# Statistic steps of an encoder layer moved along the matmul queue, two MLP products interleaved, one statistic in another PSUM bank

## The chip, the cores and the metric

The kernel runs on one core of one Trainium2 chip. The metric is the device time of one execution in microseconds, as the median of repeated runs. The engines are named as in the profile: PE is TensorE (its weight loads are listed as PEld), DVE is VectorE, ACT is ScalarE, POOL is GpSimd and SP is SyncE, which here only issues transfers.

## What is computed

One layer of an encoder on a sequence of 512 tokens of width 2048, all in float32:

```python
xn = rms_norm(x, attn_norm_g)
u_val, u_gate, q, k, v = split(xn @ w_in)
y_conv = silu(layer_norm(depthwise_conv31(u_val * sigmoid(u_gate)), ln_g, ln_b))
y_na = neighborhood_attention(q, k, v, rpb)          # 16 heads, windows of 8 x 16 on an 8 x 64 grid
mixed = concat([rms_norm(y_conv, conv_out_g), rms_norm(y_na, na_out_g)])
x = x + mixed @ w_out
xn = rms_norm(x, ffn_norm_g)
gate, val = split(depthwise_conv3(xn @ w_up))
x = x + (silu(gate) * val) @ w_down
return rms_norm(x, final_norm_g)
```

So the layer has several statistics over the channels of a token: the first norm, the mean and the variance of the LayerNorm behind the convolution, the norm of the convolution group, that of the attention group, the second norm (ahead of the MLP) and the last one.

## The kernel before, in words

**Layout.** Channels lie on the 128 partitions and tokens on the free axis, so an activation is a list of tiles of 128 x 512. Nearly all of them come from one pool with the tag "t2k" (79 buffers, made by `t2`, L85). A float32 product is taken as three products of rounded parts (`mm3`, L123: high by high, high by low, low by high; L126 to L128). Weights come in units of 128 x 1024: SP loads one (raw, L110), ACT rounds it (whi, L115), DVE takes the rest (wlo, L116). `weights()` keeps three units ahead of the one in use. A unit of an input projection is 24 matmuls of 512 columns.

**Order of the stages.** The input projections come in the order of `ORDER` (L51): convolution channels, values, and eight pairs of heads (first queries, then keys; two units each). Then the output projection runs over the convolution group (`out_half(ma, ...)`, L603), then over the attention group (L712), then the MLP (L845). Its first four hidden blocks use `up_apart` (L778): seven products of 24 matmuls of 256 columns. They are called c0 to c6 here. c6 accumulates in the PSUM bank "po", the others in turn in the three banks "mm". DVE or ACT reads each product out: c0 and c1 at L794, c2 at L796, c3 at L797, c4 at L798, c5 at L801, c6 at L802.

**Steps.** What isn't a big product is written as Python generators, and `tick` (L133) advances each of them by one step at the end of every unit: first those in `steps` (attention, the norms), then those in `asteps` (the convolution group). What a step issues on PE may not stand in PE's queue ahead of the matmul after which the tick was called. On the other engines the tick only gives the step its place in program order.

**Queues.** Each engine works through a fixed queue. The queues are laid down before the run by a planner that goes through time with its own costs and gives each engine the earliest instruction of the program that is ready by then. So a matmul of a statistic stands where the planner thought that its input was there; if the input is later on the chip, PE waits, and all the products behind it wait too. Where a line's first write to a tile of the t2k pool stands, it stands in the order of the program: no tile of that pool is first written ahead of one that the program writes first earlier.

**PSUM.** Eight banks: three "mm", two "tr", one "po", and "sc" with two. "po" takes in turn the attention output (L508), all statistics (L176 and L216), the mean of the convolution group (L398) and c6.

**A statistic** (`rsqrt_steps`, L171): four (times two passes) small matmuls sum the squares over the channels (L183), a short chain on DVE and ACT makes 1/sqrt (L186 to L193), DVE spreads it on two diagonals (dg, L213), and behind one `yield` two matmuls copy it to all partitions (L218) and ACT reads them out (L220).

**The convolution group** (`group_a`, L390) starts when the fifth head pair has been projected. Its steps, one for each unit that follows: two empty steps; the sum of the eight tiles (L394, L396); the mean (L399, L401), subtraction (L404) and squares (L405); an empty step; the matmuls of the variance (name rln); its spreading, then multiplication (L411), Silu (L412), splitting (L413) and squares (L415) of all eight tiles; five empty steps (`RA_AFTER`); the group's norm (name ra) in two steps.

**Attention** (`attention`, L525), for each head pair: a step that loads the bias tables (tab, L460); a step with the values product of the pair before (L514), the scores (L472) and the softmax (L482 to L489, Exp on ACT); three units later the transposes (trp, L499), copied out by ACT (pt, L504).

**The second norm** (`stats2`, L654): SP loads two sums of squares that POOL's transfers accumulated in DRAM (L656, L657); a step later DVE adds them and the statistic rstd2 follows. The MLP blocks multiply by it (L817, L818).

Of the kernel before, what the change touches and what calls it, by code (L numbers as in the profile page):

```python
# [10 lines left out]
F32 = mybir.dt.float32  # L11
F32R = mybir.dt.float32r
AF = mybir.ActivationFunctionType
# [3 lines left out]
P = 128  # L17
D = 2048
S = 512
# [12 lines left out]
NC_ = CONV // P  # L32
NP_ = HEADS // 2
NF = FF // P
U = 8
# [5 lines left out]
H = S // 2  # L41
# [9 lines left out]
ORDER = "aavaav" + "aq" * 4 + "qqqq"  # L51
NORM_AT = 4
NG = GW // 8
RA_AFTER = 5

PCOLS = [("g1", KD), ("dww", NC_ * CK), ("dwb", NC_), ("lng", NC_), ("lnb", NC_), ("cog", NC_),
         ("nag", NC_), ("g2", KD), ("fww", 2 * NF * 3), ("fwb", 2 * NF), ("g3", KD)]
# [9 lines left out]
def layer(ctx: ExitStack, tc: tile.TileContext, xT, xG, w_in, w_v, w_out, w_up, w_down, par, tab, out):  # L67
    nc = tc.nc
# [5 lines left out]
    psm = ctx.enter_context(tc.tile_pool(name="psm", bufs=3, space=bass.MemoryType.PSUM))  # L74
    psa = ctx.enter_context(tc.tile_pool(name="psa", bufs=1, space=bass.MemoryType.PSUM))
# [9 lines left out]
    def t2(name, dt=F32):  # L85
        return tp.tile([P, S], dt, tag="t2k", name=name)
# [11 lines left out]
    def pc(name, i):  # L98
        o = POFF[name] + i
        return prm[:, o:o + 1]  # L100
# [22 lines left out]
    def mm3(ps, w, wk, mh, ml, start, stop):  # L123
        hi, lo = w[:2]
        a = slice(wk * P, (wk + 1) * P)
        nc.tensor.matmul(ps, hi[:, a], mh, start=start, stop=False)  # L126
        nc.tensor.matmul(ps, hi[:, a], ml, start=False, stop=False)  # L127
        return nc.tensor.matmul(ps, lo[:, a], mh, start=False, stop=stop)  # L128
# [4 lines left out]
    def tick(behind):  # L133
        for todo in (steps, asteps):
            while todo:
                try:
                    with tc.issue_after(behind.ins):
                        next(todo[0])
                    break
                except StopIteration:  # L140
                    todo.pop(0)
# [14 lines left out]
    def split(src, g, name):  # L156

        h, l = t2(name + "h", F32R), t2(name + "l", F32R)
        nc.scalar.activation(h, src, AF.Copy, scale=g)
        nc.vector.scalar_tensor_tensor(l, src, g, h.bitcast(F32), op0=ALU.mult, op1=ALU.subtract)  # L160
        return h, l

    def sum_sq(acc, src, first, to=slice(0, S)):
        if first:
            nc.scalar.activation(acc, src, AF.Square)
        else:
            q = t2("sq")[:, to]
            nc.scalar.activation(q, src, AF.Square)
            nc.vector.tensor_add(acc, acc, q)

    def rsqrt_steps(accs, n, name, to=slice(0, S), keep=True, by_token=None):  # L171

        if not isinstance(accs, tuple):
            accs = accs,
        m = (to.stop - to.start) // P
        banks = [psa.tile([P, S], F32, tag="po", name="st")]  # L176
        if len(accs) > 1:
            banks.append(psa.tile([P, 2, S], F32, tag="sc", name="st")[:, 0])
        v, r, y = (sm.tile([P, S // P], F32, tag="rs" + c, name="rs" + c)[:, :m] for c in "vry")
        for b, acc in enumerate(accs):  # L180
            ps = banks[b][:, :m]
            for i in range(m):
                nc.tensor.matmul(ps[:, i:i + 1], acc[:, to.start + i * P:to.start + (i + 1) * P], ones[:, 0:1],  # L183
                                 start=True, stop=True)
            if b:
                nc.vector.scalar_tensor_tensor(v, ps, 1.0 / n, v, op0=ALU.mult, op1=ALU.add)  # L186
            else:
                nc.vector.tensor_scalar(v, ps, 1.0 / n, EPS, op0=ALU.mult, op1=ALU.add)
        nc.scalar.activation(r, v, AF.Sqrt)
        nc.vector.reciprocal(r, r)  # L190
        nc.vector.scalar_tensor_tensor(y, r, -0.5, r, op0=ALU.mult, op1=ALU.mult)
        nc.vector.tensor_mul(y, y, v)
        nc.vector.scalar_tensor_tensor(y, y, 1.5, r, op0=ALU.add, op1=ALU.mult)  # L193

        if by_token is not None:
            by_token.append(y)
# [12 lines left out]
        nc.vector.tensor_sub(yl, y, yh.bitcast(F32))  # L209
        ds = []  # L210
        for part in (yh.bitcast(F32), yl):
            ds.append(t2("dg", F32R))
            nc.vector.tensor_mul(ds[-1].rearrange("p (i k) -> p i k", k=P), ident.unsqueeze(1).broadcast_to([P, m, P]),  # L213
                                 part.unsqueeze(2).broadcast_to([P, m, P]))
        yield
        ps = psa.tile([P, S], F32, tag="po", name="st")  # L216
        for i, dg in enumerate(ds):
            nc.tensor.matmul(ps, ones_r, dg, start=i == 0, stop=i == 1)  # L218
        res = t2(name)
        nc.scalar.activation(res, ps, AF.Copy)  # L220
        return res
# [30 lines left out]
    ps = psa.tile([P, 2, S], F32, tag="sc", name="idle")  # L252
# [22 lines left out]
    for step in ORDER:  # L275
# [5 lines left out]
        i = next(a_ if step == "a" else q_)  # L281
# [106 lines left out]
    ma, ra = [], []  # L388

    def group_a():  # L390
        yield
        yield
        acc = t2("acc")
        nc.vector.tensor_add(acc, ys[0], ys[1])  # L394
        for i in range(2, NC_):
            nc.vector.tensor_add(acc, acc, ys[i])  # L396
        yield
        ps = psa.tile([P, S], F32, tag="po", name="st")  # L398
        nc.tensor.matmul(ps, ones, acc, start=True, stop=True)  # L399
        mu = t2("mu")  # L400
        nc.vector.tensor_scalar(mu, ps, 1.0 / CONV, None, op0=ALU.mult)  # L401
        acc = t2("acc")
        for i in range(NC_):
            nc.vector.tensor_sub(ys[i], ys[i], mu)  # L404
            sum_sq(acc, ys[i], i == 0)  # L405
        yield
        yield
        r = yield from rsqrt_steps(acc, CONV, "rln")
        acc = t2("acc")
        for i in range(NC_):  # L410
            nc.vector.tensor_mul(ys[i], ys[i], r)  # L411
            nc.scalar.activation(ys[i], ys[i], AF.Silu, scale=pc("lng", i), bias=pc("lnb", i))  # L412
            ma.append(split(ys[i], pc("cog", i), "ma"))  # L413
        for i in range(NC_):
            sum_sq(acc, ys[i], i == 0)  # L415
        for _ in range(RA_AFTER):
            yield

        ra.append((yield from rsqrt_steps(acc, CONV, "ra")))


# [125 lines left out]
    p, n = -1, 0  # L547
# [100 lines left out]
    rstd2 = []  # L648
# [5 lines left out]
    def stats2():  # L654
        acc2, q = t2("acc2"), t2("sq")
        nc.sync.dma_start(acc2, sq2[0])  # L656
        nc.sync.dma_start(q, sq2[1])  # L657
        yield
        nc.vector.tensor_add(acc2, acc2, q)
        rstd2.append((yield from rsqrt_steps(acc2, D, "rstd2")))  # L660

    def factors(f):

# [47 lines left out]

    out_half(mb, after)  # L712
    steps.append(stats2())

    def up(f, between):
# [61 lines left out]

    def up_apart(f, between):  # L778

        def product(c):  # L780
            w = weights()
            ps = (psa.tile([P, S], F32, tag="po", name="pu") if c == 6 else
                  psm.tile([P, S], F32, tag="mm", name="pu"))[:, :H]
            for k in range(U):
                m = comb[c][k]
                i = mm3(ps, w, k, m[:, :H], m[:, H:], k == 0, k == U - 1)
            tick(i)
            between(c)
            return ps

        vv, v, uu, g = (t2(n).rearrange("p (i t) -> p i t", i=2) for n in ("vv", "vl", "uu", "g"))
        both = lambda x: x.unsqueeze(1).broadcast_to([P, 2, H])
        for i in range(2):
            nc.scalar.activation(vv[:, i], product(i), AF.Copy)  # L794
        u, u2 = uu[:, 0], uu[:, 1]
        add(v, vv, both(product(2)))  # L796
        nc.scalar.activation(u, product(3), AF.Copy)  # L797
        add(u2, u, product(4))  # L798
        add(v, v, both(u2))
        add(vv[:, 1], vv[:, 1], u2)  # L800
        add(g[:, 0], u, product(5))  # L801
        add(g[:, 1], vv[:, 1], product(6))  # L802
        return tuple(t.rearrange("p i t -> p (i t)") for t in (g, v))
# [54 lines left out]
    n = CH  # L858
# [146 lines left out]
```

## Time and profile before

| what | us |
|---|---|
| time, median of 3 runs | 2044.64 (2043.89 to 2045.69) |
| the profiled execution, its own time | 2047.1 |
| its span, first to last instruction | 2045.3 |
| PE busy | 2025.5 |
| DVE busy | 1672.8 |
| ACT busy | 1035.4 |
| mean granted PE clock | 0.996 |

The span is the time between the first and the last instruction of one profiled execution; 1.8 us of its own time lie outside it. The profile gives a start and a duration for every instruction; an idle time of an engine is put down to what released it. PE's matmuls overlap, so a matmul of 512 columns has a duration of 0.39 us but the next one starts 0.23 us later. A row of the timeline has start, duration, engine, line, operation, out<-in, shape and count, and in square brackets the idle time before it and its releaser.

### The profile page before, as it was taken

To read this page: it belongs to the slowest core of one execution; us is meant where nothing else is said; L and a number is where in the kernel's file an instruction comes from. 1 tells how busy PE (TensorE), PEld (TensorE's weight loads), DVE (VectorE), ACT (ScalarE), POOL (GpSimd) and SP (SyncE) were. 2 spreads that over 40 slices of the span, in tenths; PEclk is the share of its full clock that TensorE was granted. 3 is DMA by queue.
4 is the path that set the end of the run, shared out by engine and by line. 5 is a ranking of instruction groups with operands and counts; after the bars stand their busy time and mean duration, and the time that the engine had idled before them with its cause. 6 is when DMAs were issued, how large, how long until landed. Compare 5 with 4: busy or idle time off the path is not lost.

```text
span 2045.3 us, 28399 instructions
## 1 busy us (share of the span) xinstructions
PE 2025.5 (99%) x10752; PEld 1731.9 (85%) x10752; DVE 1672.8 (82%) x2319; ACT 1035.4 (51%) x1662; POOL 156.2 (8%) x186
## 2 busy tenths in 40 slices
PE   9999999999999999999999999999999999999997
PEld 7888888878888898888888888888888888888887
DVE  7986888878577898888888788788888888889876
ACT  6323234347346555555555555555554555555552
POOL 0000000000001001111111111111111111110110
PEclk9999999999999999999999999999999999999998
DMA  7232333336347435566566565665555566555682
GB/s 254 82 104 91 114 95 103 108 119 216 104 121 178 113 114 144 118 151 145 124 144 144 135 133 145 138 134 142 131 146 143 124 146 146 130 134 127 149 212 83
DMA packets 97209, 275.38 MB, mean 135 GB/s; under 512 B 10928, under 2 KB 11696, under 8 KB 97072
## 3 DMA queue, kind: packets, MB, share of 16 engines
q1 hardware_dynamic: 71712, 227.40, 36.6%
q0 software_dynamic: 25216, 46.15, 15.6%
q8 instruction: 85, 1.39, 0.3%
q14 instruction: 52, 0.43, 0.1%
q10 hardware_dynamic: 144, 0.01, 0.0%
HBM read 218.99 MB, written 54.53 MB: 134 GB/s over the span
## 4 chain that ended last, share of the span: by engine, by line
PE 95%; DVE 2%; ACT 1%; DMA 1%; issue 1%; SPq 0%; DVEq 0%; ACTq 0%
PE pu L723 25%; PE pu L728 13%; PE pd L128 8%; PE pd L126 8%; PE pd L127 8%; PE pj L128 5%; PE pj L127 5%; PE pj L126 5%; PE po L126 3%; PE po L127 3%; PE po L128 3%; PE pv L330 1%; PE pv L332 1%; PE pv L331 1%; PE pu L126 1%; PE pu L128 1%
## 5 line engine op out<-in xcount | busy, mean ns | idle before, releaser
L115 ACT ACTIVATE whi<-raw 128x1024 fp32r<-128x1024 f32 x364 | 384.9, 1059 | 506.2 <-PE pj L127 148.0
L116 DVE TENSOR_TENSOR wlo<-raw,whi 128x1024 fp32r<-128x1024 f32 x364 | 443.9, 1221 | 215.6 <-ACT whi L115 205.9
L723 PE MATMUL pu<-xc,whi 128*128 128x512 f32 x2240 | 574.9, 392 | 0.2 <-ACT pl L735 0.2
L723 PEld LDWEIGHTS pu<-xc,whi 128*128 128x128 f32 x2240 | 409.2, 189 | 74.3 <-ACT pl L735 0.5
L728 PEld LDWEIGHTS pu<-xc,wlo 128*128 128x128 f32 x2240 | 305.6, 190 | 21.9
L728 PE MATMUL pu<-xc,wlo 128*128 128x256 f32 x2240 | 312.3, 282 | 0.0
L128 PE MATMUL pd<-hh,wlo 128*128 128x512 f32 x640 | 249.2, 391 | 0.0
L127 PE MATMUL pd<-hl,whi 128*128 128x512 f32 x640 | 249.2, 389 | 0.0
L126 PE MATMUL pd<-hh,whi 128*128 128x512 f32 x640 | 248.9, 391 | 0.0
L842 POOL DMA_DIRECT2D x2d<-pdc x160 | 139.2, 872 | 1169.6 <-ACT pdc L841 1051.5
L127 PE MATMUL pj<-xl,whi 128*128 128x512 f32 x512 | 200.4, 391 | 0.1
L128 PE MATMUL pj<-xh,wlo 128*128 128x512 f32 x512 | 200.0, 391 | 0.0
L126 PE MATMUL pj<-xh,whi 128*128 128x512 f32 x512 | 198.6, 392 | 0.4 <-ACT xh L267 0.4
L735 ACT ACTIVATE pl<-pu 128x256 f32<-128x256 f32 x280 | 104.4, 382 | 168.6 <-PE pu L723 168.5
L115 ACT ACTIVATE whi<-ws 128x1024 fp32r<-128x1024 f32 x132 | 139.6, 1058 | 76.9 <-PE pu L723 55.3
L384 DVE SCALAR_TENSOR_TENSOR y<-ch,prm,y 128x500 f32<-128x500 f32 (+14 forms) x240 | 173.4, 741 | 4.5
L116 DVE TENSOR_TENSOR wlo<-ws,whi 128x1024 fp32r<-128x1024 f32 x132 | 160.8, 1218 | 19.7 <-ACT whi L115 19.6
L128 PEld LDWEIGHTS pd<-hh,wlo 128*128 128x128 f32 x640 | 120.1, 188 | 28.8 <-DVE wlo L116 3.0
L127 PEld LDWEIGHTS pd<-hl,whi 128*128 128x128 f32 x640 | 120.3, 188 | 25.0
L126 PEld LDWEIGHTS pd<-hh,whi 128*128 128x128 f32 x640 | 120.5, 188 | 21.9
L841 ACT ACTIVATE pdc<-pd 128x512 f32<-128x512 f32 x160 | 93.8, 588 | 84.1 <-PE pd L128 84.1
L126 PEld LDWEIGHTS pj<-xh,whi 128*128 128x128 f32 x512 | 96.0, 188 | 22.3 <-issue 1.7
(188 smaller groups left out, 2911.3 us busy)
## 6 DMA issues: line engine op xcount, KB each, us to landing
raw<-in_w_up SPq DMA_DIRECT2D x176, 512.0 KB, 3.7
raw<-in_w_down SPq DMA_DIRECT2D x88, 512.0 KB, 4.0
x2d<-pdc POOLq DMA_DIRECT2D x160, 256.0 KB, 4.8
raw<-in_w_in SPq DMA_DIRECT2D x60, 512.0 KB, 3.7
raw<-in_w_out SPq DMA_DIRECT2D x32, 512.0 KB, 3.7
raw<-in_w_v SPq DMA_DIRECT2D x16, 512.0 KB, 4.0
tab<-in_tab SPq DMA_DIRECT2D x32, 256.0 KB, 5.1
x<-in_xG SPq DMA_DIRECT2D x16, 256.0 KB, 5.3
```

The source lines that it names most:

```text
L115: i = nc.scalar.activation(hi[:, :n], raw[:, :n], AF.Copy)
L116: j = nc.vector.tensor_sub(lo[:, :n], raw[:, :n], hi[:, :n].bitcast(F32))
L126: nc.tensor.matmul(ps, hi[:, a], mh, start=start, stop=False)
L127: nc.tensor.matmul(ps, hi[:, a], ml, start=False, stop=False)
L128: return nc.tensor.matmul(ps, lo[:, a], mh, start=False, stop=stop)
L330: nc.tensor.matmul(ps, xh, wh[:, f], start=kk == 0, stop=False)
L384: nc.vector.scalar_tensor_tensor(y[:, a:b], h[:, a + j - PAD:b + j - PAD], prm[:, o + j:o + j + 1], y[:, a:b], op0=ALU.mult, op1=ALU.add)
L723: return nc.tensor.matmul(ps, w[0][:, k * P:(k + 1) * P], comb[c][k], start=k == 0, stop=k == U - 1)
L728: nc.tensor.matmul(ps[:, H:], w[1][:, k * P:(k + 1) * P], comb[c][k][:, :H], start=False, stop=False)
L735: nc.scalar.activation(to, ps, AF.Copy)
L841: nc.scalar.activation(t, ps, AF.Copy)
L842: nc.gpsimd.dma_start(xd[d], t, accum_op=ALU.add)
```

## The change

All of it is in the order of steps, save for one bank:

- `group_a`: the two empty steps at the start go. A step's end is put into the loop of subtractions, after the fourth tile. The squares of the finished tiles move into the loop that makes them, and that loop ends a step after every second tile. `RA_AFTER` goes from 5 to 2. The number of steps up to the group's norm stays the same (12).
- `rsqrt_steps` gets two arguments. With `free` its two banks are taken from "sc" in place of "po". `rest` is the number of steps between the first and the second half.
- `stats2`: one more empty step ahead of the statistic, which is called with `free=True, rest=3`.
- `up_apart`: for the first hidden block the first two products are written as seven of eight parts of c0, seven of c1, then the last part of each; the ticks of c0 and c1 stand behind their seventh parts. Reading out c0 and c1 follows both.

```diff
-RA_AFTER = 5
+RA_AFTER = 2
...
-    def rsqrt_steps(accs, n, name, to=slice(0, S), keep=True, by_token=None):
+    def rsqrt_steps(accs, n, name, to=slice(0, S), keep=True, by_token=None, free=False, rest=1):
...
-        banks = [psa.tile([P, S], F32, tag="po", name="st")]
+
+        def bank():
+            if free:
+                return psa.tile([P, 2, S], F32, tag="sc", name="st")[:, 0]
+            return psa.tile([P, S], F32, tag="po", name="st")
+
+        banks = [bank()]
...
-        yield
-        ps = psa.tile([P, S], F32, tag="po", name="st")
+        for _ in range(rest):
+            yield
+        ps = bank()
...
     def group_a():
-        yield
-        yield
         acc = t2("acc")
...
         for i in range(NC_):
             nc.vector.tensor_sub(ys[i], ys[i], mu)
             sum_sq(acc, ys[i], i == 0)
+            if i == NC_ // 2 - 1:
+                yield
         yield
         yield
         r = yield from rsqrt_steps(acc, CONV, "rln")
...
             ma.append(split(ys[i], pc("cog", i), "ma"))
-        for i in range(NC_):
             sum_sq(acc, ys[i], i == 0)
+            if i % 2:
+                yield
         for _ in range(RA_AFTER):
             yield
-
...
         nc.vector.tensor_add(acc2, acc2, q)
-        rstd2.append((yield from rsqrt_steps(acc2, D, "rstd2")))
+        yield
+        rstd2.append((yield from rsqrt_steps(acc2, D, "rstd2", free=True, rest=3)))
...
+        def begin(c):
+            return weights(), (psa.tile([P, S], F32, tag="po", name="pu") if c == 6 else
+                               psm.tile([P, S], F32, tag="mm", name="pu"))[:, :H]
+
+        def part(c, w, ps, ks):
+            for k in ks:
                 m = comb[c][k]
                 i = mm3(ps, w, k, m[:, :H], m[:, H:], k == 0, k == U - 1)
-            tick(i)
+            return i
+
+        def product(c):
+            w, ps = begin(c)
+            tick(part(c, w, ps, range(U)))
             between(c)
             return ps
 
+        def first_two():
+            got = [begin(c) for c in range(2)]
+            for c in range(2):
+                tick(part(c, *got[c], range(U - 1)))
+            for c in range(2):
+                part(c, *got[c], range(U - 1, U))
+            return [ps for _, ps in got]
+
...
-        for i in range(2):
-            nc.scalar.activation(vv[:, i], product(i), AF.Copy)
+        for i, ps in enumerate(first_two() if f == 0 else map(product, range(2))):
+            nc.scalar.activation(vv[:, i], ps, AF.Copy)
```

More of the change, by code (lines that the diff above doesn't have):

```diff
@@ L778, in up_apart @@
     def up_apart(f, between):
[L780 to L784, printed above, removed]
+        def begin(c):
[3 more added lines that the diff above has]
+            for k in ks:
                 m = comb[c][k]
                 i = mm3(ps, w, k, m[:, :H], m[:, H:], k == 0, k == U - 1)
-            tick(i)
+            return i
+        def product(c):
+            w, ps = begin(c)
+            tick(part(c, w, ps, range(U)))
             between(c)
             return ps
+        def first_two():
[5 more added lines that the diff above has]
+            return [ps for _, ps in got]
         vv, v, uu, g = (t2(n).rearrange("p (i t) -> p i t", i=2) for n in ("vv", "vl", "uu", "g"))
         both = lambda x: x.unsqueeze(1).broadcast_to([P, 2, H])
-        for i in range(2):
-            nc.scalar.activation(vv[:, i], product(i), AF.Copy)
+        for i, ps in enumerate(first_two() if f == 0 else map(product, range(2))):
+            nc.scalar.activation(vv[:, i], ps, AF.Copy)
         u, u2 = uu[:, 0], uu[:, 1]
```

## The prediction

> **What bounds the kernel now.** I read the page first, then PE's list of waits, then PE's timeline at the waits that the change touches, and last DVE's and ACT's timeline there.
>
> ```profile
> span 2045.3 us, 28399 instructions
> ...
> PE 2025.5 (99%) x10752; PEld 1731.9 (85%) x10752; DVE 1672.8 (82%) x2319; ACT 1035.4 (51%) x1662; POOL 156.2 (8%) x186
> ```
>
> PE is busy for 99% of the span, and the change takes no product away. It can gain only where PE stands still, and what it can lose is a new standstill. The list of PE's waits (engine, line, releaser; total, times, longest) has six that lie in the changed stretches:
>
> ```profile
> PE st L399 <- DVE acc L396: 1.3, 1, 1.3
> PE st L218 <- DVE dg L213: 1.1, 1, 1.1
> ...
> PE trp L499 <- DVE tab L489: 0.9, 1, 0.9
> PE pu L126 <- ACT xc L612: 0.8, 1, 0.8
> PE pu L126 <- ACT rstd L220: 0.7, 1, 0.7
> ...
> PE st L183 <- DVE acc L659: 0.4, 1, 0.4
> ```
>
> Together 5.2 us, by starts and ends of a matmul's record. What a wait costs is seen better from start to start, since the next matmul normally starts 0.23 us after the last:
>
> ```profile
> 426.19 0.39 PE L126 MATMUL pj<-xh,whi 128*128 128x512 f32 x1
> ...
> 432.31 0.39 PE L126 MATMUL pj<-xh,whi 128*128 128x512 f32 x1
> 434.02 1.10 PE L399 MATMUL st<-acc,ones 128*128 128x512 f32 x2 [1.32 <-DVE acc L396]
> ...
> 478.87 0.39 PE L127 MATMUL pj<-xl,whi 128*128 128x512 f32 x1
> 480.17 0.63 PE L499 MATMUL trp<-ident,tab 128*128 128x128 f32 x4 [0.91 <-DVE tab L489]
> ```
>
> From 426.19 to 432.31 PE starts 27 matmuls, 0.227 us apart; a unit of 24 lasts 5.44 us. The mean's matmul starts 1.71 us after its predecessor, so 1.48 us are lost; the transposes' wait costs 1.30 - 0.23 = 1.07 us. At the second norm:
>
> ```profile
> 691.06 0.28 PE L128 MATMUL pu<-xc,wlo 128*128 128x256 f32 x1
> 692.47 1.01 PE L218 MATMUL st<-dg,ones 128*128 128x512 f32 x2 [1.14 <-DVE dg L213]
> 694.17 0.39 PE L126 MATMUL pu<-xc,whi 128*128 128x256 f32 x1 [0.69 <-ACT rstd L220]
> ```
> ```profile
> 694.17:698.05 3.88, 3.88 (x20) 3.88 (x20) 0.82 (x2) 0.23 (x1) 0.56 0.00 0
> 698.05:720.00 21.95, 21.95 (x185) 21.95 (x184) 2.27 (x5) 1.09 (x3) 1.00 0.31 97
> ```
>
> The second fence is the product tiles by stretches (length, PE, PEld, DVE, ACT, then the granted clock, DMA share, GB/s). The last matmul of c4 gives way at 691.18, and the next product starts at 694.17: 2.99 us, of which the two spreading matmuls need 2 x 0.23. So 2.53 us are lost. Then the clock is granted at 0.56, and 20 matmuls take 3.88 us where the next stretch needs 21.95 / 185 = 0.119 us for one, 2.37 us in all: 1.51 us more. **The second norm loses 4.0 us here**, more than the list of waits says.
>
> **The convolution group.** What it adds up does not grow: the same additions, subtractions, squares and splits, the same 12 steps to the group's norm. Only their places move. PE's first step and DVE before:
>
> ```profile
> 404.58 1.47 PE L499 MATMUL trp<-ident,tab 128*128 128x128 f32 x12
> ```
> ```profile
> 402.75 0.73 DVE L384 SCALAR_TENSOR_TENSOR y<-ch,prm,y 128x497 f32<-128x497 f32 x1
> ...
> 412.14 0.69 DVE L433 TENSOR_TENSOR q<-pj,rstd 128x512 f32<-128x512 f32 x1 [5.28 <-PE pj L128]
> ...
> 419.58 0.68 DVE L394 TENSOR_TENSOR acc<-y 128x512 f32<-128x512 f32 x1
> ...
> 421.38 2.48 DVE L482 SCALAR_TENSOR_TENSOR tab<-sc,tab 128x512 f32<-128x512 f32 x4
> ...
> 431.86 0.68 DVE L489 TENSOR_TENSOR tab<-tab,su 128x512 f32<-128x512 f32 x1
> 432.46 1.41 DVE L396 TENSOR_TENSOR acc<-acc,y 128x512 f32<-128x512 f32 x2
> ```
>
> The convolution is done at 403.5, yet the sum of its tiles starts at 419.58, in the third step, and is squeezed between the softmax until 433.87, past PE's arrival at 432.54. With the two empty steps gone it belongs to the first step, behind the transposes that PE starts at 404.6. DVE then is free for 5.28 us ahead of 412.14; seven additions at 0.6 (their starts in a row) need 4.3. The mean's matmul stands behind the second step, which ends at about 412. I take its wait as 0; at the worst it is what it is now, 1.48, at the best there is no more to gain. The mean's own matmuls cost the same in either place.
>
> What is late next is the sum of squares of the variance. The four subtractions of the second step lie in idle DVE time before the scores; the last four additions share the softmax's stretch, four where there were six, so they end two additions (1.2 us) before 433.87, at 432.7; PE comes to them behind the fifth step, at 432.3 plus the mean's 1.2, 433.5. No wait by 0.8 us, narrowly. The bound is again 1.48.
>
> ```profile
> 447.71 0.95 PE L183 MATMUL st<-ones,acc 128*128 128x1 f32 x8
> ...
> 456.07 0.66 PE L514 MATMUL po<-pt,vg 128*64 128x128 f32 x8
> ...
> 457.97 2.00 PE L472 MATMUL sc<-k,q 64*128 64x256 f32 x16
> ...
> 474.77 0.60 PE L499 MATMUL trp<-ident,tab 128*128 128x128 f32 x4
> ```
> ```profile
> 455.35 0.58 ACT L220 ACTIVATE rln<-st 128x512 f32<-128x512 f32 x1
> 455.95 1.28 ACT L412 ACT_TABLE_LOAD   x1
> ...
> 467.41 1.28 ACT L487 ACT_TABLE_LOAD   x1
> ```
> ```profile
> 479.34 1.28 DVE L489 TENSOR_TENSOR tab<-tab,su 128x512 f32<-128x512 f32 x2
> ```
> ```profile
> 450.46 2.05 SPq L460 DMA_DIRECT2D tab<-in_tab  x4
> ```
>
> The variance moves from 447.71 to about 433.5, rln from 455.35 to about 444. Between 456 and 475 the eight Silus, splits and squares now run ahead of the Exps of a softmax, and PE meets its third transposes late (tab until 480.6). Its scores now end at 459.97; the values product ahead of them waits for rln's read of "po" (455.93), about 1.8 us that go, as do the mean's 1.5, so they end near 456.7. With the Silus done by then, that softmax needs what it needed in the pair before, 421.38 to 432.54, 11.2 us, and some two more for the second half of the splits: ready by 470, where the first transposes are due at 474.77 - 1.5, about 473. The 1.07 us go, with some 3 us to spare. Bounds: nothing gained, 0, and one new pair of table loads, 2 x 1.28, lies inside the spare time. The tables for that softmax (SP, 450.46) now stand behind the first writes of rln and of the first two splits, which by the same reckoning are made by about 450 (rln 444, a table load, two Silus with their splits and squares at some 2 us each): no later than now.
>
> **The second norm.** The second load of `stats2` on SP's queue:
>
> ```profile
> 683.38 0.32 SPq L657 DMA_DIRECT2D sq<-sq  x1
> ```
>
> It is issued when POOL's last accumulating transfer has landed; the step doesn't hold it, so a tick that is three matmuls earlier doesn't move it, and PE's 0.4 us for L659 stay. No transfer is moved past another on SP's or POOL's queue.
>
> The interleaving of c0 and c1:
>
> ```profile
> 674.20:679.24 5.04, 5.04 (x43) 5.04 (x42) 0.00 (x0) 0.00 (x0) 1.00 0.88 235
> ```
>
> 43 matmuls run ahead of the wait for xc, which are 2 x 21 and one of c2: the planner already puts c1's seven parts ahead of c0's last. Writing that order out costs and gains 0; the bounds are the 0.8 us of that wait, gained or lost again.
>
> What counts is `rest=3` and the bank. The spreading matmuls now stand behind c5, 24 matmuls later; DVE's diagonals are long there. c6 no longer shares "po" with rstd2. But c5 needs a bank "mm", which DVE frees by reading c2 (L796):
>
> ```profile
> 692.25 0.68 DVE L213 TENSOR_TENSOR dg<-ident,rsl 128x512 fp32r<-128x512 f32 x1
> ...
> 693.98 0.68 DVE L796 TENSOR_TENSOR vl<-vv,pu 128x512 f32<-128x512 f32 x1
> ```
> ```profile
> 693.52 0.60 ACT L220 ACTIVATE rstd<-st 128x512 f32<-128x512 f32 x1 [1.15 <-PE st L218]
> ```
>
> c2's products had ended two products earlier, yet its reading out starts only behind rstd2's: the order of first writes in the t2k pool. In the new program rstd2 comes behind c5, so L796 follows the second diagonal at about 692.85 and ends at 693.5. Meanwhile PE takes c6. How many of its matmuls stand ahead of c5 is the planner's guess of 1.2 us of DVE work (half of a diagonal and L796), some 10 x 0.12; then PE waits from 691.18 + 1.2 = 692.4 to about 693.6: **1.2 us remain.** Bounds: 0 (c6 whole in front) and 2.4 (none). With a standstill of 1.2 I expect full clock, since behind the mean's 1.48 the clock stays at 1.00:
>
> ```profile
> 436.00:446.00 10.00, 10.00 (x52) 8.41 (x51) 10.00 (x16) 7.15 (x12) 0.00 (x0) 1.00 0.18 52
> ```
> Behind that wait stand c5, the spreading matmuls and the rest of c6, so it costs its full length. Sum here: 4.0 - 1.2 = 2.8 gained. Who waits for the later rstd2 are L817 and L818 and behind them the next block's first copies; c5 ends near 696.5 (24 x 0.12 on) and rstd2 at 697.6, ahead of c6's end, and the banks that are then free last for the next block's first three products, 8.6 us.
>
> **The rule on the clock.** The trace shows half clock after a stretch of 2.99 us in which PE ran only two matmuls, and none after one of 1.48 us. [...]
>
> **The sum.** 1.48 + 1.07 + 2.8 = 5.35 us. Against the profiled execution, 2047.1 - 5.35 = 2041.75 (span 2039.95). It is 2.46 above the median, so of the median 2044.64 remain **2039.3 us**. What a measurement of this kernel can tell from no change is about 0.2%, 4.1 us: the line is at 2040.5.
>
> **The rivals.**
> - *The standstills only move in the group* (14%): the mean's 1.48 reappears at the variance, and the transposes wait as now. For it: DVE's queue between 421 and 434 is full and the planner is optimistic there. Gain 2.8: 2041.8.
> - *The wait for c5's bank takes the place of rstd2's* (9%): PE's queue has c5 at once, waits 2.4 and gets half clock. Gain at the norm 4.0 - 2.4 - 1.5 = 0.1; in all 2.65: 2042.0. Against it: c6 has a free bank and is ready.
> - *The half clock stays whatever the standstill* (7%): 2039.3 + 1.5 = 2040.8. For it: PE wasn't wholly idle in the 2.99 us.
> - *It doesn't do what it says* (3%): the steps give only a lower bound on places, and the queues stay nearly as they are: 2044.6.
> - *No remainder either* (8%): c5's wait goes too: 2038.1.
> - *Slower* (4%): ACT. Silu and Exp each had a table load of 1.28 us, once. The eight Silus now come in four steps; if they alternate with the eight Exps of the softmax behind 456, up to 14 more loads, 17.9 us, less 3 to spare, delay the transposes: 14.9 lost against 4.3 gained, 2055.2. It decides from nine more loads on. Against it: a Silu writes in place and needs only rln, so all eight are ready before the scores. [...]
>
> The forecast has 55%. Its own error of about a microsecond leaves a quarter of it above 2040.5. So **faster** (over 0.2%) is 41 + 8 and some of the third rival, 52%; **slower** 4%; within 0.2% 44%. Range, 8 in 10: from 2037.6 (2038.1 and half a microsecond for the small waits at xc and L659) to 2042.4 (only one of the two parts works, 2041.8 to 2042.0, and some error).
>
> **What would show it.** Right: no wait of PE for L396 near 412; the variance's matmuls near 433 without one; no wait at L499 near 472; L218 of rstd2 behind c5; a wait of some 1.2 us for L796; clock 1.00 throughout 690 to 700; still only one Silu and one Exp load between 440 and 475. Wrong: a row of PE waiting for L169 or L412, more ACT_TABLE_LOAD rows, or a stretch with clock below 1 behind 690.

## The result and the profile after

| | before | after |
|---|---|---|
| median, us (10 runs each) | 2045.62 (2043.89 to 2046.74) | 2040.29 (2038.82 to 2041.88) |
| span of the profiled execution, us | 2045.3 | 2039.1 |

The ratio of the times is 0.9973, with a 95% interval of 0.9965 to 0.9982: 5.3 us less, between 3.7 and 7.2. The forecast was 5.35 us less. As the sections below show, the direction and the stages were right, the mechanism at the second norm was in part wrong, and the size came out so well by luck, because errors in it offset each other.

The lines of the changed file stand 5 to 21 lines lower than before: the mean is L404, the variance L189, the diagonals L219, the spreading matmuls L225, reading out a statistic L227, the transposes L506; c2 is read out at L817 and the second norm's sum is L666.

First the page's span and engines, and then PE's list of waits (engine, tile, line and what it waited for; total, times, longest), both of the changed kernel:

```profile
span 2039.1 us, 28396 instructions
...
PE 2023.6 (99%) x10752; PEld 1730.6 (85%) x10752; DVE 1672.1 (82%) x2319; ACT 1035.5 (51%) x1662; POOL 156.6 (8%) x186
```
```profile
PE rb L210 <- DVE dg L206: 1.9, 1, 1.9
PE idle L261 <- DVE warm L258: 1.6, 1, 1.6
PE st L189 <- DVE acc L169: 0.9, 1, 0.9
PE pu L126 <- ACT xc L619: 0.8, 1, 0.8
PE pu L731 <- ACT pl L743: 0.6, 1, 0.6
PE st L189 <- DVE acc L666: 0.4, 1, 0.4
```

The four waits that the change was after (for L396, L489, L213 and L220 of before) are gone, and no new one is in the list: the others are in before's too. The wait for xc and the one for the second norm's sum have stayed. Two marks divide the span: PE's first matmul of the MLP and its first wide product. They are the first starts in the rows of the tile pu:

```profile
L731 PE MATMUL pu<-xc,whi x2240: 387/389/499, 755.2 to 1953.8; 128*128 128x512 f32 x187
...
L126 PE MATMUL pu<-xc,whi x224: 278/283/386, 671.6 to 754.9; 128*128 128x256 f32 x112
```

| stage, from start to start | before | after | less |
|---|---|---|---|
| **group**: transposes at 404 to the MLP's first matmul | 404.58 to 674.20: 269.62 | 404.16 to 671.61: 267.45 | 2.17 |
| **norm**: the MLP's first matmul to the first wide one | 87.81 | 83.64 | 4.17 |

At the transposes at 404 the changed kernel is already 0.42 us earlier, by a wait for xh at the start that this execution of before had; behind the second mark it loses 0.6 us, at products that are the same in both. The two stages tell where the change works, and the single times and medians don't: the stretch from the first wide product to the last alone took 1197.3 to 1199.5 us over the traces of this study.

In the group, PE's timeline (start, duration, engine, line, out<-in, shape, count), DVE's and ACT's:

```profile
412.43 1.02 PE L404 MATMUL st<-acc,ones 128*128 128x512 f32 x2
...
432.57 0.39 PE L128 MATMUL pj<-xh,wlo 128*128 128x512 f32 x1
432.98 1.02 PE L189 MATMUL st<-ones,acc 128*128 128x1 f32 x8
...
473.05 1.47 PE L506 MATMUL trp<-ident,tab 128*128 128x128 f32 x12
```
```profile
432.16 0.67 DVE L169 TENSOR_TENSOR acc<-acc,sq 128x512 f32<-128x512 f32 x1
...
467.21 0.68 DVE L496 TENSOR_TENSOR tab<-tab,su 128x512 f32<-128x512 f32 x1
```
```profile
443.75 1.28 ACT L419 ACT_TABLE_LOAD   x1
...
458.87 1.28 ACT L494 ACT_TABLE_LOAD   x1
```

The mean has no bracket any more, nor have the transposes, whose table was ready at 467.89, 5.2 us ahead of them. The variance starts 0.41 us after the matmul before it, where 0.23 is usual: its last addition ended at 432.83. Silu and Exp have one table load each.

At the second norm, PE's timeline from the last matmul of c4 to the first of c5, DVE's with ACT's reading of c3 (L818), and the stretch as a whole (length, PE, granted clock, DMA share, GB/s):

```profile
688.45 0.28 PE L128 MATMUL pu<-xc,wlo 128*128 128x256 f32 x1
...
690.13 0.39 PE L225 MATMUL st<-dg,ones 128*128 128x512 f32 x1
...
690.71 0.39 PE L225 MATMUL st<-dg,ones 128*128 128x512 f32 x1
690.93 0.28 PE L127 MATMUL pu<-xc,whi 128*128 128x256 f32 x1
691.05 0.28 PE L126 MATMUL pu<-xc,whi 128*128 128x256 f32 x1
```
```profile
689.03 0.68 DVE L219 TENSOR_TENSOR dg<-ident,rsh 128x512 fp32r<-128x512 f32 x1
689.64 0.68 DVE L219 TENSOR_TENSOR dg<-ident,rsl 128x512 fp32r<-128x512 f32 x1
689.67 0.36 ACT L818 ACTIVATE uu<-pu 128x256 f32<-128x256 f32 x1
690.24 0.68 DVE L817 TENSOR_TENSOR vl<-vv,pu 128x512 f32<-128x512 f32 x1
```
```profile
690.00:694.00 4.00, 4.00 (x34) 1.00 0.08 33
```

Between c4 and c5 stand 13 matmuls of c6, a spreading matmul, three of c6, the other spreading matmul and one of c6. They fill the 2.5 us in which DVE makes the diagonals and reads c2. DVE is no faster than before: the first diagonal starts 4.8 us after the variance's matmuls in both kernels. PE stands nowhere, and the clock stays at 1.00.

### The profile page after: what moved, and what is told of

It reads as the page before. It is cut to its first block, busy times and chain, and to the rows that moved or that the text cites. A ratio compares the mean times of both kernels' runs of the same rounds, so it can differ in the third digit from the quotient of the medians.

```text
span 2039.1 us, 28396 instructions
## 1 busy us (share of the span) xinstructions
PE 2023.6 (99%) x10752; PEld 1730.6 (85%) x10752; DVE 1672.1 (82%) x2319; ACT 1035.5 (51%) x1662; POOL 156.6 (8%) x186
## 4 chain that ended last, share of the span: by engine, by line
PE 97%; issue 1%; DVE 1%; DMA 0%; ACT 0%; POOL 0%; DVEq 0%; ACTq 0%; POOLq 0%; SPq 0%
PE pu L731 25%; PE pu L736 13%; PE pd L128 8%; PE pd L126 8%; PE pd L127 8%; PE pj L126 6%; PE pj L128 6%; PE pj L127 6%; PE po L126 3%; PE po L127 2%; PE po L128 2%; PE pv L339 1%; PE pv L338 1%; PE pv L337 1%; PE pu L128 1%; PE pu L126 1%
```

## The experiments

For each kernel the two stages are given, and two terms of the second one: the waits for xc and for L666 (from start to start, less the usual 0.12), which change from one execution to the next, and the stage without them. Where the table says "under 0.12", nothing is taken off.

| kernel | ratio to before, 95% interval | group | norm | xc | L666 | norm without both |
|---|---|---|---|---|---|---|
| before | | 269.62 | 87.81 | 0.93 | 0.57 | 86.31 |
| after | 0.9973 (0.9965 to 0.9982) | 267.45 | 83.64 | 0.97 | 0.52 | 82.15 |
| e1_group | 0.9988 (0.9979 to 0.9997) | 267.51 | 87.91 | 0.94 | 0.68 | 86.29 |
| e2_norm | 0.9986 (0.9978 to 0.9995) | 269.68 | 82.88 | 0.46 | 0.26 | 82.16 |
| e3_rest1 | 0.9975 (0.9965 to 0.9985) | 267.53 | 85.61 | 0.58 | 1.38 | 83.65 |
| e4_po_bank | 0.9980 (0.9971 to 0.9989) | 267.53 | 84.79 | 1.01 | under 0.12 | 83.78 |
| e5_bank_alone | 0.9973 (0.9963 to 0.9983) | 267.49 | 83.13 | 0.76 | under 0.12 | 82.37 |
| e6_no_step | 1.0008 (0.9999 to 1.0017) | 267.51 | 89.26 | 0.95 | 2.22 | 86.09 |
| e7_three_and_later | 0.9981 (0.9972 to 0.9990) | 267.47 | 85.09 | under 0.12 | under 0.12 | 85.09 |
| e8_light | one run, 2044.42 | 267.46 | 87.31 | 1.02 | under 0.12 | 86.29 |
| e9_all_covered | 0.9979 (0.9970 to 0.9988) | 267.49 | 84.46 | under 0.12 | under 0.12 | 84.46 |
| e10_no_spreading | one run, 2044.02 | 267.88 | 87.02 | 0.80 | under 0.12 | 86.22 |
| e11_only_spreading | one run, 2053.14 | 279.01 | 85.73 | 0.98 | under 0.12 | 84.75 |
| e12_changed_again | 0.9974 (0.9963 to 0.9984) | 267.47 | 83.61 | 0.93 | 0.53 | 82.15 |

### The two parts alone

e1: of the change only the group's part, that is the edits of `RA_AFTER` and `group_a`.

> Only the group's part of the change: the two empty steps gone, squares and Silus spread over steps, RA_AFTER 2; the second norm and the first block's products as before. Theory (two separate parts): the waits of 1.48 and 1.07 us go, less 0.2 to 0.4 that the variance and small changes of the queue take back, as between the two traces: from the transposes at 404 to the first product of the MLP 267.4 us instead of 269.6; then the second norm still stands for 2.99 us with half clock behind it, 87.8 us from the first product to the first wide one. In all 2.2 less than before. Rival (the standstills only move): the stage stays within half a microsecond of 269.6 and the time within 0.5 of before.

e2: only the rest of it, the edits of `rsqrt_steps`, `stats2` and `up_apart`.

> Only the second norm's part: the scores' bank, the longer rest, the extra step, the first two products written out; the group as before. Theory: the 2.53 us of standstill and the 1.51 us of half clock both go and nothing takes their place: 83.6 to 83.8 us from the first product to the first wide one instead of 87.8, and 269.6 from the transposes at 404 to the first product. In all 4.0 to 4.2 less than before. Rival (the prediction's remainder): 1.2 us stay as a wait of c5 for the reading of c2, 85.0 us, 2.8 less in all.

Both hold by their stages. The group's part gives 2.1 us wherever it is (267.45 to 267.53 in all kernels that have the whole of it, 269.62 and 269.68 in the two that lack it), and does nothing to the norm. The norm's part takes 4.15 us off the norm's stage (86.31 to 82.16), and nothing is left of the remainder of 1.2 us; e2's stage is even shorter than the 83.6 to 83.8 expected, because both of its waits happened to be short. By the medians the two parts bring 1.6 and 2.7 us; the intervals are too wide to add to this.

### What carries the gain at the second norm

e3, the rest back at one step:

```diff
-rsqrt_steps(acc2, D, "rstd2", free=True, rest=3)
+rsqrt_steps(acc2, D, "rstd2", free=True)
```

> The changed kernel with rest back at 1. On PE's queue 13 matmuls of c6, a spreading matmul, 3, the other one and 4 more stand ahead of c5 (13, 3 and 1 in the changed kernel). Theory (the bank carries it): with the statistic in the scores' bank c6 need not wait for any reading of it, and fills the time of the diagonals; the rest does nothing. 83.6 to 83.8 us from first product to first wide one, clock 1.00, the time within 0.5 us of the changed kernel. Rival (the rest carries it, as the prediction reasons): the spreading matmuls come back to where they stood, 2.5 us of standstill and 1.5 of half clock come back: 87.8 us for the stage, 4 us more.

e4, the bank back at po:

```diff
-rsqrt_steps(acc2, D, "rstd2", free=True, rest=3)
+rsqrt_steps(acc2, D, "rstd2", rest=3)
```

> The changed kernel with the statistic back in the bank po; rest stays at 3. On PE's queue both spreading matmuls stand right behind c4, then c5, then c6. Theory (the bank carries it): PE waits some 1.1 us for the diagonals and then for the bank of c5 or for rstd2, as before: 2.5 us of standstill, and behind it the clock falls again, 1.5 us: the stage takes 87.0 to 88.2 us, the time is 3.5 to 4.5 us above the changed kernel. Rival (the rest carries it): the stage stays at 83.6 to 84.0 us. Rival on the clock: the standstill is back and the clock stays at 1.00: 86.1 to 86.5 us.

e5, the group's part and the bank alone:

```diff
-        yield
-        rstd2.append((yield from rsqrt_steps(acc2, D, "rstd2", free=True, rest=3)))
+        rstd2.append((yield from rsqrt_steps(acc2, D, "rstd2", free=True)))
...
-enumerate(first_two() if f == 0 else map(product, range(2)))
+enumerate(map(product, range(2)))
```

> The group as in the changed kernel, and of the second norm's edits the bank alone: rest 1, no extra step, the first two products not written out. On PE's queue stand 13 matmuls of c6, a spreading matmul, 3, the other one and 8 more ahead of c5. Theory (the bank carries the gain there): no standstill behind c4 and clock 1.00; the stage from the first product to the first wide one takes 83.6 us, give or take what the wait for L666 happens to be (0.1 to 1.4 us in the runs so far), the time is that of the changed kernel within 0.6 us. Rival (rest, extra step and order are needed too): some of the 2.53 and 1.51 us come back, 85 to 87.9 us.

The timeline behind c4, first in e4, with DVE's reading of c2 (L817), then in e5, with the weight load of c5's first matmul (PEld):

```profile
687.54 0.28 PE L128 MATMUL pu<-xc,wlo 128*128 128x256 f32 x1
688.96 1.01 PE L225 MATMUL st<-dg,ones 128*128 128x512 f32 x2 [1.14 <-DVE dg L219]
689.33 0.68 DVE L817 TENSOR_TENSOR vl<-vv,pu 128x512 f32<-128x512 f32 x1
689.80 0.28 PE L126 MATMUL pu<-xc,whi 128*128 128x256 f32 x1
```
```profile
690.80 0.28 PE L128 MATMUL pu<-xc,wlo 128*128 128x256 f32 x1
691.10 0.19 PEld L126 LDWEIGHTS pu<-xc,whi 128*128 128x128 f32 x1 [0.22 <-ACT uu L817]
691.10 0.39 PE L126 MATMUL pu<-xc,whi 128*128 128x256 f32 x1
```

With the bank po the spreading matmuls stand right behind c4 and wait for the diagonals as before (1.42 us from start to start, 0.12 usual: 1.30), and from the first of them to c5 another 0.84 - 0.45 = 0.39 go, most of it at the second diagonal. That is 1.7 us, and 83.78 - 82.15 = 1.63. With the bank alone, e5, c6 fills this time, and 0.18 us are left at c5, until ACT has read c3 (L817 of e5): 82.37 against 82.15. So the theory of the bank holds: c6's bank is po, and a statistic that takes po too keeps c6 out until ACT has read it. Rest, extra step and written order add only 0.2 us to the bank. But e4 lost less than expected. Its standstill is 1.7 us, not 2.5, because there c5 stands ahead of c6 and needn't wait for the reading of rstd2, and the clock stayed at 1.00. So these three edits without the bank still bring 2.5 us (86.31 to 83.78), 1.5 of them by the clock; the two ways overlap, and the bank alone brings nearly all.

e3's theory holds for the queue, and its stage is 1.5 us too long in another place. Its wait for L666 happened to be 1.38 us, and behind it the clock fell (stretches, columns as above):

```profile
683.40:684.90 1.50, 0.30 (x3) 1.00 0.10 38
684.90:686.70 1.80, 1.78 (x15) 1.00 0.00 0
686.71:690.12 3.41, 3.41 (x18) 0.50 0.81 234
690.12:692.00 1.88, 1.88 (x18) 1.00 0.35 142
```

The half clock doesn't follow the wait at once: PE works for 1.8 us at 1.00 first.

### The order of the first products

e6, the changed kernel without the extra step in `stats2`:

```diff
         nc.vector.tensor_add(acc2, acc2, q)
-        yield
```

> The changed kernel without the extra step in stats2. With the first two products written out, the ticks come earlier, and the variance's matmuls L189 stand 24 matmuls (2.9 us) earlier on PE's queue than in the changed kernel, right behind the first 20 of the third product. Theory (writing the order out is free only with the extra step): PE waits there for L666, 2.9 us longer than the 0.4 of the changed kernel, some 3.3 us, and the clock falls behind it, 1.5 us more: the stage takes 87 to 88 us, the time is 3 to 4.5 us above the changed kernel. Rival (as the prediction has it: a tick that is a few matmuls earlier moves nothing): 83.6 us, no more than half a microsecond above the changed kernel.

```profile
681.76 0.28 PE L128 MATMUL pu<-xc,wlo 128*128 128x256 f32 x1
684.10 1.75 PE L189 MATMUL st<-ones,acc 128*128 128x1 f32 x8 [2.06 <-DVE acc L666]
686.38 0.58 PE L126 MATMUL pu<-xc,whi 128*128 128x256 f32 x1 [0.53 <-ACT whi L115]
...
687.64 0.58 PE L128 MATMUL pu<-xc,wlo 128*128 128x256 f32 x1 [0.47 <-DVE wlo L116]
```

The theory holds, with other sizes. The variance stands 20 matmuls earlier (not 24, as the expectation has it) and waits 2.22 us. Behind it PE takes c6 first, for whose weights it waits another 1.0 us (0.53 and 0.47), and the clock is at a half for 6.8 us, from 684.3 to 691.1. All the gain of the change is lost. So writing out the first two products gains nothing by itself (e5 does without it and is as fast); it moves the ticks, and the extra step in `stats2` is what makes that harmless.

### Whether the clock follows idle time

e8, the second norm's one-column matmuls four times over:

```diff
-            for i in range(m):
+            for i in list(range(m)) * (4 if free else 1):
```

> The changed kernel in which the second norm's eight one-column matmuls (by the trace's count) are done four times over, with the same sums: 24 more at 0.115 us, 2.8 us of PE that is never idle and does hardly any work. Theory (the clock follows what share of some 3.3 us PE's array works): these light matmuls count for little, and about 3.3 us behind their start the clock falls to a half for some 3.4 us: 1.5 us more, so the stage takes 83.6 + 2.8 + 1.5 = 87.9 us. Rival (only idle time counts): the clock stays at 1.00, 86.4 us.

The variance's matmuls in e8 (duration least/median/most in ns, first and last start), and then two stretches of its PE:

```profile
L189 PE MATMUL st<-ones,acc x32: 212/250/313, 683.9 to 687.3; 128*128 128x1 f32 x32
```
```profile
683.97:687.38 3.41, 3.41 (x33) 1.00 0.41 123
687.38:690.80 3.42, 3.42 (x17) 0.50 0.31 73
```

PE is busy without a gap, and the clock falls all the same, from 687.4 to 690.8. The stage without both waits is 86.29: 82.15, the 24 light matmuls (2.7 us), and 1.5. The theory holds in this run: the clock fell behind 3.41 us of one-column matmuls in which PE was never idle. The 3.3 us of the expectation lie between the 3.2 us (e3) and 3.4 us (before, e1) that passed in the traces ahead of it between the standstill and the half clock; here it is 3.5 us.

### The parts of the group

e10, only the two empty steps gone:

> Of the group's edits only the two empty steps are gone; subtractions with squares in one step, Silus and squares in one step, RA_AFTER 5; the second norm as before. The mean stands where it does in the changed kernel, the variance 24 matmuls (5.4 us) earlier than there, ra's statistic 14 us earlier. Theory (the spreading is what keeps the additions from being late): PE waits for the variance's last addition or the softmax behind it is late: of the 2.13 us that the whole part brings, a microsecond or more is lost again, 268.5 us or more from the transposes at 404 to the MLP's first product. Rival (the two empty steps are the whole part): 267.5 us.

e11, only the spreading and `RA_AFTER`:

> Of the group's edits only the spreading and RA_AFTER 2; the two empty steps are kept, the second norm as before. The mean stands where it stood before. Theory (the places of the sums decide): the mean's 1.48 us stay, and the transposes, whose softmax has the later Silus beside it, come no earlier: 269.6 us or up to 1.5 more for the stage. Rival (spreading alone frees the softmax's stretch): the 1.07 us of the transposes go, 268.5 us.

e10's theory falls. The group's stage is 267.88, 0.4 us longer than with the spreading; one wait came in, for rln's diagonals, at which 0.74 us go:

```profile
436.73 0.47 PE L225 MATMUL st<-dg,ones 128*128 128x512 f32 x1 [0.58 <-DVE dg L219]
```

So the two empty steps carry 1.75 of the 2.15 us. e11 is far beyond both expectations: the mean's wait stays, and the stage is 9.4 us longer than before, lost at the group's norm. There PE first waits for the bank po, out of which ACT reads the attention output only behind its Exps, then 2.90 us for the diagonals and 1.41 for the next bank. The row of PE's timeline, and ACT's table loads:

```profile
505.00 1.18 PE L189 MATMUL st<-ones,acc 128*128 128x1 f32 x8 [2.81 <-ACT ao L529]
```
```profile
458.69 1.28 ACT L496 ACT_TABLE_LOAD   x1
462.59 1.28 ACT L421 ACT_TABLE_LOAD   x1
464.79 1.28 ACT L496 ACT_TABLE_LOAD   x1
468.80 1.28 ACT L421 ACT_TABLE_LOAD   x1
```

Here Exp (L496) and Silu (L421) do take turns: the slow rival of the prediction, in a kernel whose Silus come two steps later than in the changed one. The two extra loads are 2.6 us of ACT; how much of the 9.4 us they cause wasn't separated. Part of it is the clock, which is at a half for 10.2 us there, from 505.8 to 516.0.

### Two tries at the waits that stay

e7, three products written out instead of two, and one step more ahead of the variance:

```diff
+        yield
         rstd2.append(...)
...
-            got = [begin(c) for c in range(2)]
+            got = [begin(c) for c in range(3)]
```

> The changed kernel with three products written out in place of two (63 matmuls ahead of the first that needs the last xc, in place of 42) and one step more ahead of the second norm's variance. Theory (both remaining waits are a matter of place): the wait for xc, 0.97 us from start to start, and the one for L666, 0.52, go; 13 to 24 matmuls stand behind where the diagonals are needed, so no new wait comes; the stage takes 82.0 to 82.3 us and the time is 1.4 to 1.5 us below the changed kernel, 6.5 to 7 below the kernel before. Rival (the later statistic is late for the second block): PE waits for a reading that needs rstd2 behind c6, and the stage stays at 83.6 us or longer.

e9, the same with two steps more, rest 1, and c3 in a bank "tr":

> The changed kernel with three products written out, the fourth one's bank taken from tr so that it needn't wait for the reading of the first, two steps more ahead of the second norm's variance, and rest 1. On PE's queue 63 matmuls stand ahead of the first that needs the last xc, the variance 28 matmuls (3.4 us) later than in the changed kernel, and the spreading matmuls behind the second product of the next block. Theory (the last two waits are a matter of place, and nothing else is late then): the 0.97 us for xc and the wait for L666 (0.52 in the changed kernel's trace) go, no wait comes in: 82.1 to 82.3 us from the first product to the first wide one, 1.0 to 1.5 us below the changed kernel. Rival (the later rstd2 is late for what follows): a new wait behind 690, and the stage stays at 83.1 us or longer.

In both the waits for xc and L666 are gone, and others are there. In e7 the fourth product waits 1.69 us for one of the three banks mm, all of which are held by three products that haven't been read out, and the spreading matmuls wait 1.20. In e9, behind 690:

```profile
698.65 1.02 PE L225 MATMUL st<-dg,ones 128*128 128x512 f32 x2 [0.23 <-DVE dg L219]
700.72 0.36 PE L126 MATMUL pu<-xc,whi 128*128 128x256 f32 x1 [1.05 <-DVE g L826]
703.98 0.39 PE L126 MATMUL pu<-xc,whi 128*128 128x256 f32 x1 [0.17 <-ACT vv L819]
```

From start to start these lose 2.3 us, more than the 1.5 gained: e9's rival holds, e7's theory falls. Neither is better than the changed kernel, which gave 0.9974 beside e9.

e12, the changed kernel again:

> The changed kernel once more, beside the others on their chip. The stage of the group takes 267.5 us, as in the traces so far; the second norm's stage 82.9 to 83.7 us by what the waits for xc and L666 happen to be; if the clock's fall depends on where a window of some 3.4 us lies, it may also show it once behind L666 (85 us).

It shows the same stages, 267.47 and 83.61, and no fall of the clock.

## Why the prediction was right, and where it was not

**Group, 2.55 forecast, 2.13 to 2.17 measured.** The mean's 1.48 and the transposes' 1.07 are gone as reckoned (the mean behind 412, the table ready at 468 where 470 was forecast, one Silu and one Exp load). Of the missing 0.4 us, 0.18 are the variance: the spare 0.8 us didn't exist, since PE came to it at 432.8, not 433.5, while the addition ended at 432.83 as forecast (432.7). The other 0.2 were not traced. Of the rival that the standstills only move, the mean's 1.48 that reappears at the variance, an eighth came true.

**Order of c0 and c1, 0 forecast.** Right for the whole: 43 matmuls ahead of the wait for xc in all of before, after and e5. The reason given, that a tick which comes a few matmuls earlier moves nothing, was wrong: without the extra step the earlier ticks cost more than the whole change brings (e6).

**Second norm, 2.8 forecast, 4.15 measured: the step that failed.** The prediction says that what counts is the rest and the bank, that the spreading matmuls stand behind c5, and that a wait of 1.2 us for c5's bank remains, until DVE has read c2. Of this only the bank is so, and alone it does nearly all (e5: 3.9 of 4.2 us). The spreading matmuls stand ahead of c5, in the midst of c6, and the remainder is 0. DVE was forecast well: the second diagonal ends and the reading of c2 ends where the prediction puts them, if both are moved up by the 2.6 us that the changed kernel is ahead there (692.85 and 693.5 forecast; 690.32 and 690.92 in the trace). What was wrong is first the length of the fill. The prediction gave it about ten matmuls of c6, 1.2 us, from a planner that has half a diagonal and L817 still to wait for; in the queue there are 17 and the two spreading matmuls, 17 x 0.12 + 2 x 0.23 = 2.5 us. With that c5 would not have waited for c2's bank either, which is free 0.13 us before c5 starts. The second error is the bank itself. In e4 c5 starts at 689.80, before DVE has read c2 (until 690.01), and in e5 what releases c5 is ACT's reading of c3; in the changed kernel's trace, too, c5's first matmul waits for ACT alone, whose reading of c3 ended at 690.03, 1.0 us before c5 starts. With the ten matmuls of the prediction some 0.3 us would have remained, not 1.2 (an estimate: 690.03 for the bank, against 688.57, where c4 gives way, + 1.2). The rival without a remainder, given 8%, was the one for this place.

**The half clock, 1.51 forecast.** It goes with the standstill, as said, so the rival that it stays falls. But before doesn't have it in every execution. The same standstill of 1.30 and 1.25 us is in before, e1, e10 and e11. In three of the four the clock falls behind it, in e11 it doesn't. First e1 at its standstill and behind it, then e11 (columns as above; the stretches are laid out as in the last section, one half clock's length each):

```profile
689.18:692.59 3.41, 1.55 (x7) 1.00 0.36 139
692.59:696.00 3.41, 3.41 (x18) 0.50 0.00 0
```
```profile
696.93:700.34 3.41, 2.81 (x24) 1.00 0.80 249
700.34:703.76 3.42, 2.16 (x12) 1.00 0.16 63
703.76:707.17 3.41, 3.41 (x31) 1.00 0.00 0
```

In e1 the whole standstill lies in one such stretch, in which PE is busy for 1.55 us; in e11 it is shared by two, with 2.81 and 2.16 us. The stage without both waits says the same, 86.2 to 86.3 against 84.75. Of the 30 runs of before beside e1 to e4, 14 had a mean granted clock of 0.996 and a median of 2046.3, 13 had 0.997 and 2044.59, 3 had 0.998 and 2043.58; half clock for 3.4 us is 0.0008 of the span. So it seems that a term that is there in about half of the executions was counted in full. That these runs differ by this very fall is argued from their clock; it isn't shown, as only the profiled ones have traces.

**The sum.** Between the two profiled executions the change brings 2.17 + 4.17, less what lies outside the stages: 6.2 us of span, where 5.35 was forecast. Of the median it brings 5.33. The profiled execution of before was a long one (2047.1), and about half of the fall of the clock isn't in the median: 2.13 + 2.53 + half of 1.5 is 5.4. So the forecast of 2039.3 came near 2040.29, and to the difference of the medians nearly exactly, by luck: a remainder of 1.2 us that isn't there stands against half of 1.51 and 0.4 of the group that aren't there either.

**Slower through table loads, given 4%.** It did not come: the changed kernel has one Silu and one Exp load of 1.28 us (443.75 and 458.87), though its Silus come in four steps. In e11, where Exp and Silu take turns, there are two of each, 2.6 us more.

## What to carry to other kernels

A statistic in a PSUM bank of its own let the products behind it run ahead of its slow chain on DVE (e5, the bank alone: 3.9 of 4.2 us); look which product shares a bank with a short job, before moving steps about. An edit that only writes out an order can move every tick behind it (e6: the variance 20 matmuls earlier, 2.22 us of wait): look where each later step's first instruction then stands on PE. And of a term that may be there in some executions only, such as a fall of the clock (behind the same standstill in three traces of four), count its share, and judge such an edit by stages from start to start in several traces: the group's stage agreed within 0.1 us where the runs of one kernel spread by 1 to 4.

## What the runs showed of the hardware

- **PE's clock fell to a half behind stretches with little work, once without any idle time.** It fell behind 1.38 us of standstill followed by eight one-column matmuls (e3), and behind 32 one-column matmuls without any gap (e8), and not behind the mean's standstill of 1.48 us with full matmuls after it (before), nor behind 1.30 and 0.39 us in e4.
- **It came late and lasted 3.41 us, or two or three times as long.** The half clock began 2.4 us (e6), 3.2 us (e3), 3.4 us (before, e1) and 3.5 us (e8) after the work stopped or became light, 1.8 us after PE had resumed in e3, and lasted 3.41 us; in e6, where PE stood again in that time, 6.83 us, and in e11's group 10.24 us. In the trace of before the changes of the clock lie 689.49, 3.413 and 1334.61 us apart, which are 202, 1 and 391 times 3.413.
- **How much work stood ahead of a fall.** Divide a trace into stretches of 3.413 us, the length of before's half clock, counted from the first change of the clock, and add up the matmuls that start in a stretch, 0.227 us for 512 columns and in proportion for fewer. Those filled to 0.30 or less were followed by half clock: in before 0.20 at the second norm, in before and after the last ones of the span (0.23 and less), and in the stages of the others 0.23 (e1), 0.27 (e3), 0.00 (e8), 0.27 and 0.10 (e6), 0.00, 0.07 and 0.20 (e11's group). Those filled to 0.40 or more were not: 0.40 at the mean's standstill and at least 0.53 in all others of before and after, 0.73 and 0.47 at e11's second norm. So the same standstill cost half a clock in e1 and nothing in e11, by how it lay across these stretches. No run moved it against them on purpose.
- **The wait for L666 varies by itself** from less than 0.12 to 1.38 us, in kernels that have the same 92 product matmuls of the MLP ahead of it; it ends with transfers (in the changed kernel's trace L666 waits 0.5 us for what SP loads, which lands 2.7 us after its issue). e3 paid for it twice: 1.38 us of wait and 1.5 us by the clock.
